# Two sums of weight blocks per MLP quad, formed by adding transfers on GpSimd in place of VectorE additions

## The chip, the cores and the metric

The kernel runs on one core of a Trainium2 chip. The metric is device time in microseconds: the median of several executions. A separate, profiled execution gives the trace. The engines are TensorE (PE; its weight loads are PEld), VectorE (DVE), ScalarE (ACT), GpSimd (POOL) and SyncE (SP). Each runs its own instructions in the order fixed at build time and waits on semaphores for the others.

## The reference, cut to what matters

A trunk of two layers works on 512 tokens of width 1024 in float32. Layer 0 mixes tokens with an mLSTM, layer 1 with a short gated convolution. Behind each mixer stands a squared-ReLU MLP with an inner width of 4096. Every part is normed before and after and added to the residual. The change touches the first matrix product of both MLPs:

```
def sqrelu_mlp(x, w_up, w_down):
    h = jax.nn.relu(x @ w_up)
    return (h * h) @ w_down
```

## The kernel before, in words

**Precision.** Every float32 factor is split into a high and a low part in the matmul's own format: `split` (L80) casts the high part on ACT (L81) and subtracts it on DVE to get the low one (L82). Each product is then three matmuls (`mm3`, L113, with the matmuls at L116 to L118): high by high, high by low, low by high.

**The up projection by quads.** `x @ w_up` is computed by a scheme of Strassen's kind that needs seven half-size products in place of eight. The rows of `w_up` (1024) are cut in two halves (`kh`), the columns into 8 groups of 512, and each group again in two halves (`nh`). One column group is a quad. It works on four blocks of 512 x 256, named in the code:

- `a` is block (0, 0), `b` is (0, 1), `c` is (1, 0) and `d` is (1, 1).

A block is 512 KB and lies in SBUF as a raw tile of 128 x 1024 (four rows of 256 columns in each partition). Raw tiles come from a pool of 7. `block` (L825) takes a raw tile and loads it from SyncE's queue (L828). `factor` (L834) takes a tile `u`, of which there are 15 for all purposes, and splits the raw tile into it. `prod` (L805) is one product of 24 matmuls of 128 x 256 into a PSUM tile `pu` (four of them). The token side of the products (`a11`, `a12`, `p1`, `r3`, `p4`, `n2`, `a22`) is prepared once per MLP by the class `Seven`.

In `run` (L854) four sums of blocks are made on DVE, in place in the raw tiles: `a + b` into `a` (L860), `b + d` into `b` (L870), then `a + d` into `a` (L877), giving a + b + d, of which the factor `w6` is made, and at last `c` added on top (L882) for the factor `w4`. Blocks `a` and `c` are also factors on their own, in `begin` (L842) and `first_done` (L849), and `d` too (L876). So `a` must have been split for the first product before the sum overwrites it, when both use the same raw tile.

**The order of the quads.** In `mlp` (L899), the first AHEAD = 3 quads are begun before their turn: their first two products (with `a` and with `c`) run from raw tiles of their own at the start of the MLP, and `run` loads the blocks again. Quads 3 to 7 are not begun: there `run` uses one raw `a` for the first product and for the sums. After quads 0 and 1, each `down(g)` (the part of the second matrix product that quad g's result feeds) alternates with the next quad. `down` accumulates in PSUM tiles `pd`, of which there are two; each result is added into SBUF by DVE (L946), or copied there by ACT when g is 0 (L944). The results of a quad's products are combined on DVE (L885 to L893), squared (L910) and split into tiles `hb`. At the end of the MLP `last_product` (L297) does the last part of the second product, and its parts on GpSimd are L338 and the power in L190.

**What orders the work.** A framework takes the instructions as the code issues them, finds the dependencies, and fixes an order for each engine when the program is built; that order need not be the code's. The constants LATE, BLOCK and PROD with `step` and `put_off` say when the transposes of a normed token tile are placed among the matmuls; the change leaves them as they are. GpSimd's queue holds, near the MLP, the power of `rstd_of` (L190), the norm gains (L177), the copies of the residual to DRAM (L796) and, before `down(5)`, the reload of that residual (L964).

Of the kernel before, what the change touches and what calls it, by code (L numbers as in the profile page):

```python
# [12 lines left out]
ALU = mybir.AluOpType  # L13

P = 128
# [25 lines left out]
def tile_hybrid_trunk(  # L41
# [15 lines left out]
    nc = tc.nc  # L57
# [10 lines left out]
    def pu():  # L68
        return psum("pu", 4)
# [24 lines left out]
    def raw_tile(shape, dtype=F32):  # L94
        return big.tile([P] + shape, dtype, tag="raw", name="raw", bufs=NRAW)
# [421 lines left out]
    def rows():  # L517
# [24 lines left out]
    a = T1[0:H, :]  # L542
    nc.vector.scalar_tensor_tensor(
        out=a, in0=thi, scalar=CAP, in1=nb, op0=ALU.mult, op1=ALU.add
# [4 lines left out]
    for c in range(NT):  # L549
# [6 lines left out]
            out=mprev[:, c + 1 : c + 2], in0=M[:, last], in1=nb[:, last], op=ALU.subtract  # L556
        )

    def by_chunk(r):
        return r.rearrange("h (c l) -> h c l", l=P)  # L560
# [3 lines left out]
        out=by_chunk(T1[32 : 32 + H, :]),  # L564
        in0=mprev[:, 0:NT].unsqueeze(2).broadcast_to([H, NT, P]),
        in1=M3,
        op=ALU.subtract,
# [3 lines left out]
        out=by_chunk(T1[96 : 96 + H, :]),  # L571
        in0=by_chunk(a),
        in1=M3[:, :, P - 1 : P].broadcast_to([H, NT, P]),
        op=ALU.subtract,
# [37 lines left out]
    for h in range(H):  # L612
# [4 lines left out]
        for c in range(NT):  # L617
# [8 lines left out]
            out=DT[:, h, :, :],  # L626
# [178 lines left out]
    def prod(o, fw, fx, first):  # L805

        for p in range(4):
            step(PROD / 4)
            for u in range(2):
                mm3(  # L810
                    o[:, u * 256 : (u + 1) * 256],
                    [fw[:, i, p, u * P : (u + 1) * P] for i in range(2)],
                    [fx[:, i, p, :] for i in range(2)],
                    first and p == 0 and u == 0,
                    p == 3,
                )

    class Quad:
# [3 lines left out]
        def __init__(self, wm, c0, c1, xT, take):  # L822
            self.wm, self.cols, self.xT, self.take = wm, (c0, c1), xT, take

        def block(self, kh, nh):  # L825
            c = self.cols[nh]
            raw = raw_tile([4, 256])
            nc.sync.dma_start(  # L828
                raw,
                self.wm[kh * 512 : (kh + 1) * 512, c : c + 256].rearrange("(p q) m -> q p m", q=P),  # L830
            )
            return raw

        def factor(self, src):  # L834
            w = unit([2, 4, 256], F32R)
            split(w[:, 0], w[:, 1], src)
            return w
# [16 lines left out]
        def run(self, begun):  # L854
            tt = nc.vector.tensor_tensor
            f = self.xT.f
            a, b = self.block(0, 0), self.block(0, 1)
            if not begun:
                self.begin(a)
            tt(out=a, in0=a, in1=b, op=ALU.add)  # L860
            w = self.factor(a)
            z = pu()
            prod(z, w, f["p1"], True)
            s1, s5 = self.s1, self.values()
            nc.scalar.copy(s5, by_tile(z))
            if not begun:
                c = self.block(1, 0)
                self.first_done(c)
            d = self.block(1, 1)
            tt(out=b, in0=b, in1=d, op=ALU.add)  # L870
            w = self.factor(b)
            y = pu()
            prod(y, w, f["r3"], True)
            s7 = self.values()
            nc.scalar.copy(s7, by_tile(y))
            w = self.factor(d)  # L876
            tt(out=a, in0=a, in1=d, op=ALU.add)  # L877
            w6 = self.factor(a)
            prod(z, w, f["p4"], False)
            if begun:  # L880
                c = self.block(1, 0)
            tt(out=a, in0=a, in1=c, op=ALU.add)  # L882
            w4 = self.factor(a)
            prod(y, w6, f["n2"], False)
            tt(out=s1, in0=by_tile(y), in1=s1, op=ALU.add)  # L885
            tt(out=s7, in0=s1, in1=s7, op=ALU.subtract)
            tt(out=s7, in0=by_tile(z), in1=s7, op=ALU.subtract)
            tt(out=s5, in0=s5, in1=s1, op=ALU.subtract)
            o = pu()
            prod(o, w4, f["a22"], True)  # L890
            self.take(1, 0, s7, None)
            self.take(1, 1, s5, None)
            tt(out=s1, in0=by_tile(o), in1=s1, op=ALU.add)  # L893
            self.take(0, 1, s1, None)

    def by_tile(o):
        return o.rearrange("p (u n) -> p u n", u=2)
# [142 lines left out]
```

## Time and profile before

| | us |
|---|---|
| median of 3 runs | 1138.42 (1138.06 to 1138.58) |
| profiled execution | 1139.16 |
| its span in the trace | 1137.4 |
| PE busy | 1098.1 (97%) |
| PEld busy | 949.2 (83%) |
| DVE busy | 733.9 (65%) |
| ACT busy | 450.2 (40%) |
| POOL busy | 64.9 (6%) |
| moved by DMA | 126.35 MB, 111 GB/s on average |

A page of the profile gives the busy time of each engine, then the span in 40 slices (one of them is 28.4 us) with a digit for the busy tenths of each, the DMA queues, the chain of work that ended last, and groups of instructions. In a group or an order of time, a row names the line of the kernel, the engine, the operation and the tiles as `out<-in`. What stands behind `<-` in brackets is what ended the idle time of the engine before that row. A busy PE need not be a PE at its peak, since matmuls are pipelined and their ends are modelled. The first MLP lies at about 244 to 560 us of the span, the second at about 785 us to the end.

### The profile page before, as it was taken

What the parts mean: (1) busy time and instruction counts of PE and PEld (TensorE: products, weight loads), DVE (VectorE), ACT (ScalarE), POOL (GpSimd) and SP (SyncE); (2) the same over time, 40 slices, a digit from 0 to 9 for tenths busy, and PEclk for the clock granted to TensorE, in tenths of its full rate; (3) what the DMA queues carried; (4) which work ended last, traced back from release to release, by engine and by line L of the source; (5) the groups of instructions that cost most, each with busy time, mean ns of one, the idle gap of its engine ahead of it and who ended that gap; (6) DMA issues with size and microseconds to landing.
All of it is one profiled execution on the core that took longest, in us unless ns stands there. A gap on an engine that the chain in (4) does not pass through costs nothing.

```text
span 1137.4 us, 15341 instructions
## 1 busy us (share of the span) xinstructions
PE 1098.1 (97%) x6243; PEld 949.2 (83%) x6243; DVE 733.9 (65%) x993; ACT 450.2 (40%) x692; POOL 64.9 (6%) x108
## 2 busy tenths in 40 slices
PE   8999999969999999999999999996999999999997
PEld 5878887869798898899889888786978889889986
DVE  5552665469776776767685444346977677676763
ACT  6431543346444244234363222234644424423421
POOL 2000100110000000000130000011000000000011
PEclk9999999989999999999999999998999999999999
DMA  8420363044353243153535331104435324315301
GB/s 263 135 67 1 101 214 93 38 158 157 117 162 96 71 130 104 64 186 103 138 88 172 113 106 59 56 37 145 151 119 160 94 74 130 104 64 185 103 28 56
DMA packets 112749, 126.35 MB, mean 111 GB/s; under 512 B 4998, under 2 KB 85158, under 8 KB 112679
## 3 DMA queue, kind: packets, MB, share of 16 engines
q1 hardware_dynamic: 109366, 113.31, 32.0%
q0 software_dynamic: 3312, 12.06, 2.9%
q8 instruction: 49, 0.80, 0.3%
q14 instruction: 22, 0.17, 0.1%
HBM read 119.07 MB, written 6.29 MB: 110 GB/s over the span
## 4 chain that ended last, share of the span: by engine, by line
PE 73%; DVE 11%; issue 9%; ACT 3%; DMA 2%; POOL 1%; SPq 0%; POOLq 0%; DVEq 0%; ACTq 0%
PE pu L116 12%; PE pu L117 12%; PE pu L118 12%; PE pd L117 11%; PE pd L118 11%; PE pd L116 11%; DVE u L82 4%; DMA raw<-in_w_in_mlstm_dram 1%; ACT u L81 1%; ACT junk L198 1%; DMA raw<-in_w_mlp_up_dram 1%; DVE t L910 1%; POOL small L190 1%; DVE u L291 1%; DVE hb L82 1%
## 5 line engine op out<-in xcount | busy, mean ns | idle before, releaser
L116 PE MATMUL pu<-u 128*128 128x256 f32 (+1 forms) x1296 | 408.2, 315 | 19.1 <-ACT u L81 18.8
L118 PE MATMUL pu<-u 128*128 128x256 f32 (+1 forms) x1296 | 403.2, 312 | 4.4 <-DVE u L82 4.4
L117 PE MATMUL pu<-u 128*128 128x256 f32 (+1 forms) x1296 | 404.8, 312 | 0.4 <-DVE u L82 0.4
L82 DVE TENSOR_TENSOR u<-raw,u 128x1024 fp32r<-128x1024 f32 (+1 forms) x248 | 295.4, 1204 | 137.7 <-ACT u L81 137.4
L81 ACT CAST u<-raw 128x1024 fp32r<-128x1024 f32 (+1 forms) x248 | 251.4, 1035 | 272.0 <-PE pd L118 118.3
L116 PEld LDWEIGHTS pu<-u 128*128 128x128 f32 x1296 | 246.0, 190 | 36.5 <-ACT u L81 20.5
L118 PEld LDWEIGHTS pu<-u 128*128 128x128 f32 x1296 | 245.1, 189 | 20.7 <-DVE u L82 6.0
L117 PEld LDWEIGHTS pu<-u 128*128 128x128 f32 x1296 | 246.0, 190 | 16.3 <-DVE u L82 1.3
L117 PE MATMUL pd<-u,hb 128*128 128x512 f32 (+1 forms) x648 | 254.2, 392 | 1.3 <-DVE u L82 1.3
L116 PE MATMUL pd<-u,hb 128*128 128x512 f32 (+1 forms) x648 | 254.5, 393 | 0.7 <-ACT u L81 0.4
L118 PE MATMUL pd<-u,hb 128*128 128x512 f32 (+1 forms) x648 | 253.9, 392 | 0.0
L117 PEld LDWEIGHTS pd<-u,hb 128*128 128x128 f32 x648 | 121.7, 188 | 30.1 <-DVE u L82 2.9
L116 PEld LDWEIGHTS pd<-u,hb 128*128 128x128 f32 x648 | 121.5, 188 | 29.3 <-DVE t L332 1.2
L118 PEld LDWEIGHTS pd<-u,hb 128*128 128x128 f32 x648 | 121.7, 188 | 28.1
L81 ACT CAST hb<-t 128x512 fp32r<-128x512 f32 x80 | 49.1, 621 | 86.1 <-DVE t L910 74.2
L946 DVE TENSOR_TENSOR u<-u,pd 128x512 f32<-128x512 f32 x80 | 54.7, 683 | 29.6 <-PE pd L118 29.5
L198 ACT ACTIVATE junk<-u 128x512 bf16<-128x512 f32 (+1 forms) x49 | 30.5, 623 | 77.7 <-DVE u L335 48.3
L82 DVE TENSOR_TENSOR hb<-t,hb 128x512 fp32r<-128x512 f32 x80 | 53.4, 687 | 3.8 <-ACT hb L81 3.6
L332 DVE TENSOR_TENSOR t<-pd,gain 128x512 f32<-128x512 f32 x16 | 11.0, 688 | 36.3 <-ACT junk L198 36.3
L964 POOL DMA_DIRECT2D u<-xd x8 | 4.3, 536 | 493.6 <-PE pu L118 493.6
L910 DVE SCALAR_TENSOR_TENSOR t<-t 128x512 f32<-128x512 f32 x48 | 31.5, 685 | 0.0
L291 DVE SCALAR_TENSOR_TENSOR u<-t,small,u 128x512 f32<-128x512 f32 (+1 forms) x33 | 22.9, 733 | 10.8 <-POOL small L190 10.8
(153 smaller groups left out, 664.8 us busy)
## 6 DMA issues: line engine op xcount, KB each, us to landing
raw<-in_w_mlp_up_dram SPq DMA_DIRECT2D x76, 512.0 KB, 3.7
raw<-in_w_mlp_down_dram SPq DMA_DIRECT2D x64, 512.0 KB, 3.5
raw<-in_w_in_mlstm_dram SPq DMA_DIRECT2D x24, 512.0 KB, 4.8
raw<-in_w_in_conv_dram SPq DMA_DIRECT2D x24, 512.0 KB, 5.3
raw<-in_w_out_mlstm_dram SPq DMA_DIRECT2D x8, 512.0 KB, 4.1
xd<-u POOLq DMA_DIRECT2D x8, 512.0 KB, 2.9
u<-xd POOLq DMA_DIRECT2D x8, 512.0 KB, 5.8
raw<-in_w_out_conv_dram SPq DMA_DIRECT2D x8, 512.0 KB, 3.5
```

Of the source, the lines that this page charges most:

```text
L81: hi = nc.scalar.copy(dst_hi, src)
L82: lo = nc.vector.tensor_tensor(out=dst_lo, in0=src, in1=dst_hi.bitcast(F32), op=ALU.subtract)
L116: nc.tensor.matmul(o, lh, rh, start=first, stop=False, skip_group_check=True)
L117: nc.tensor.matmul(o, lh, rl, start=False, stop=False, skip_group_check=True)
L118: nc.tensor.matmul(o, ll, rh, start=False, stop=last, skip_group_check=True)
L190: nc.gpsimd.tensor_tensor(out=r, in0=r, in1=mhalf[:, 0:1], op=ALU.pow)
L198: nc.scalar.activation(junk(n), src, AF.Square, scale=float(D) ** -0.5, accum_out=ms[:, i : i + 1])
L291: nc.vector.scalar_tensor_tensor(out=xt[:, hs], in0=y, scalar=r, in1=xt[:, hs], op0=ALU.mult, op1=ALU.add)
L332: nc.vector.tensor_tensor(out=yg, in0=o, in1=g[:, cs], op=ALU.mult)
L910: nc.vector.scalar_tensor_tensor(out=c, in0=o, scalar=0.0, in1=c, op0=ALU.max, op1=ALU.mult)
L946: nc.vector.tensor_tensor(out=yh, in0=yh, in1=o, op=ALU.add)
L964: nc.gpsimd.dma_start(xs[t], xd[t])
```

## The change

The sums L860 and L870 are no longer DVE additions. GpSimd issues a transfer that reads the second block from HBM once more and adds it to the raw tile: block (0, 1) onto `a`, and block (1, 1) onto `b`. The loads of `b` and `d` into raw tiles of their own remain. The sums at L877 and L882 remain on DVE. With 8 quads in each of 2 MLPs, 32 additions become 32 adding transfers of 512 KB.

```
+        def src(self, kh, nh):
+            c = self.cols[nh]
+            return self.wm[kh * 512 : (kh + 1) * 512, c : c + 256].rearrange(
+                "(p q) m -> q p m", q=P
+            )
+
         def block(self, kh, nh):
-            c = self.cols[nh]
             raw = raw_tile([4, 256])
-            nc.sync.dma_start(
-                raw,
-                self.wm[kh * 512 : (kh + 1) * 512, c : c + 256].rearrange("(p q) m -> q p m", q=P),
-            )
+            nc.sync.dma_start(raw, self.src(kh, nh))
             return raw
+
+        def plus(self, raw, kh, nh):
+            nc.gpsimd.dma_start(raw, self.src(kh, nh), accum_op=ALU.add)
...
             a, b = self.block(0, 0), self.block(0, 1)
             if not begun:
                 self.begin(a)
-            tt(out=a, in0=a, in1=b, op=ALU.add)
+            self.plus(a, 0, 1)
             w = self.factor(a)
...
             d = self.block(1, 1)
-            tt(out=b, in0=b, in1=d, op=ALU.add)
+            self.plus(b, 1, 1)
             w = self.factor(b)
```

## Prediction

> **What bounds the kernel now.** I read the page first, its busy shares and its forty slices.
>
> ```profile
> span 1137.4 us, 15341 instructions
> ...
> PE 1098.1 (97%) x6243; PEld 949.2 (83%) x6243; DVE 733.9 (65%) x993; ACT 450.2 (40%) x692; POOL 64.9 (6%) x108
> ...
> PE   8999999969999999999999999996999999999997
> ...
> DVE  5552665469776776767685444346977677676763
> ```
>
> TensorE is busy for 97% of the span, so VectorE time is worth something only near the few slices where PE falls under 9. Counted from 0, PE falls to 6 in slices 8 and 27, and DVE reaches its only 9s in the slices right behind, 9 and 28: the starts of the two MLPs. The table of windows sizes them.
>
> ```profile
> core 0: us, PE busy (x) PEld busy (x) DVE busy (x) ACT busy (x) POOL busy (x), PEclk, DMA share, GB/s
> 260.00:300.00 40.00, 36.90 (x285) 34.53 (x283) 37.73 (x49) 18.95 (x28) 0.00 (x0) 1.00 0.46 145
> 300.00:330.00 30.00, 29.43 (x168) 25.49 (x169) 19.79 (x20) 17.85 (x24) 0.00 (x0) 1.00 0.52 160
> 330.00:400.00 70.00, 70.00 (x409) 61.36 (x408) 52.57 (x64) 24.10 (x28) 0.00 (x0) 1.00 0.26 83
> 400.00:470.00 70.00, 70.00 (x463) 63.91 (x462) 52.86 (x63) 27.72 (x34) 0.00 (x0) 1.00 0.35 113
> 800.00:840.00 40.00, 37.58 (x297) 35.85 (x296) 37.73 (x50) 19.58 (x29) 0.00 (x0) 1.00 0.45 143
> 840.00:900.00 60.00, 59.34 (x327) 50.60 (x326) 43.71 (x50) 26.00 (x33) 0.00 (x0) 1.00 0.35 109
> ```
>
> In the 40 us behind each start DVE works for 37.73 us and PE idles for 3.10 and 2.42 us. In the 140 us from 330 on PE is busy for all of it and DVE for three quarters: a faster DVE gives nothing there. The chain of waits says which DVE work sets PE's pace at the first start.
>
> ```profile
> 272.25 0.15 DVE raw L860
> 272.40 0.98 issue
> 273.39 1.22 DVE raw L882
> 274.61 1.14 DVE raw L870
> 275.74 2.34 DVE u L82 x2
> ```
>
> Quad 1's two sums (L860, L870) lie in the chain, around quad 0's last sum (L882), whose factor (L82) PE is about to need.
>
> **What the change removes.** Each quad loses one L860 and one L870.
>
> ```profile
> L860 DVE TENSOR_TENSOR raw<-raw x16: 1215/1220/1226, 254.8 to 1056.2; 128x1024 f32<-128x1024 f32 x16
> L870 DVE TENSOR_TENSOR raw<-raw x16: 1218/1225/1228, 256.3 to 1058.2; 128x1024 f32<-128x1024 f32 x16
> ```
>
> That is 32 x 1.22 = 39 us of DVE, off 733.9. Almost all of it lies where PE has no idle time and pays nothing. What pays is quad 1's pair in each start: in the chain they take 0.15 + 0.98 = 1.13 us and 1.14 us, together 2.27 us, twice 4.5 us. It cannot be much more: all of PE's idle time in the four windows around the starts is 3.10 + 0.57 + 2.42 + 0.66 = 6.8 us. Behind the removed sums L82 and L882 stay next on DVE, then PE itself, so I count no more than the two pairs. Quad 0's pair stands ahead of the saturated stretch, at 254.8 and 256.3; I count it at nothing, since its replacements arrive later than it did. The loads on SP stay as they are: both blocks that are now added by a transfer are still loaded too, since later sums and factors read them.
>
> **What it adds.** 32 transfers of 512 KB on GpSimd's queue, 16.8 MB more reading. The trace has no adding transfer. The nearest rows are the plain loads that GpSimd issues (L964) and SP's loads of the same blocks.
>
> ```profile
> raw<-in_w_mlp_up_dram SPq DMA_DIRECT2D x76, 512.0 KB, 3.7
> ...
> u<-xd POOLq DMA_DIRECT2D x8, 512.0 KB, 5.8
> ```
>
> ```profile
> L964 POOL DMA_DIRECT2D u<-xd x8: 527/531/577, 489.2 to 1033.0; - x8
> ...
> DMA to landing us min/median/max: 4.0/5.8/6.8
> ```
>
> Call X the time from the issue of an adding transfer to its landing. From below, X is no less than 3.7 us, SP's load of the same block. From above, I take twice 5.8 = 11.6 us, as if reading the tile were a second transfer in series. I take 7.4: the 5.8 of GpSimd's own load, plus three more issue times of 0.53 us, since a block is 512 rows of 1 KB where that tile is 128 rows of 4 KB; it is nearest to that row. Against 1.22 us on DVE the sum thus comes some 6 us later after its inputs.
>
> The Trainium skill, DMA: Bandwidth & Descriptors, section "Anatomy of one DMA", fits a transfer from GpSimd as 2.0 us plus bytes over 436 GB/s, an estimate of 3.2 us here; the 5.8 of this trace disagrees and decides, and by 3.2 no wait below would appear and the sum would stay at -4.5 us. The Trainium skill, Collectives: The Full Stack, section "The bandwidth ceiling", speaks against the change: an adding transfer has two sources to read where a copy has one. No run here shows that yet; by it, 5.8 plus another 1.2 us for 512 KB at that rate is an estimate of 7.0, and the hold worked out below would be 1.2 us in place of 1.6.
>
> **Where the later sum is hidden.** Quads 0 to 2 were begun ahead: nothing else reads `a` before the sum, so the transfer can go as soon as the tile is in. In quads 3 to 7 the transfer into `a` must first wait until L81 and L82 have split the raw `a` for the first product. The one into `b` waits for `b` alone, no longer for L860. Quad 4 of the first MLP, on DVE:
>
> ```profile
> 380.60 1.22 DVE L82 TENSOR_TENSOR u<-raw,u 128x1024 fp32r<-128x1024 f32 x1
> ...
> 382.93 1.23 DVE L860 TENSOR_TENSOR raw<-raw 128x1024 f32<-128x1024 f32 x1
> 384.19 1.23 DVE L870 TENSOR_TENSOR raw<-raw 128x1024 f32<-128x1024 f32 x1
> 385.33 0.68 DVE L946 TENSOR_TENSOR u<-u,pd 128x512 f32<-128x512 f32 x1
> 385.93 1.22 DVE L82 TENSOR_TENSOR u<-raw,u 128x1024 fp32r<-128x1024 f32 x1
> ...
> 388.61 0.68 DVE L946 TENSOR_TENSOR u<-u,pd 128x512 f32<-128x512 f32 x1
> ...
> 393.31 0.69 DVE L946 TENSOR_TENSOR u<-u,pd 128x512 f32<-128x512 f32 x1 [1.15 <-PE pd L118]
> 396.09 0.69 DVE L946 TENSOR_TENSOR u<-u,pd 128x512 f32<-128x512 f32 x1 [2.09 <-PE pd L118]
> ...
> 399.74 0.68 DVE L946 TENSOR_TENSOR u<-u,pd 128x512 f32<-128x512 f32 x1
> ```
>
> ```profile
> 322.96 0.59 ACT L865 COPY t<-pu 128x512 f32<-128x512 f32 x1 [0.70 <-PE pu L118]
> 325.80 0.59 ACT L875 COPY t<-pu 128x512 f32<-128x512 f32 x1 [1.31 <-PE pu L118]
> ...
> 384.27 1.05 ACT L81 CAST u<-raw 128x1024 fp32r<-128x1024 f32 x1 [3.52 <-DVE raw L860]
> ```
>
> The split of `a` ends at 381.8. A transfer issued then lands at 381.8 + 7.4 = 389.2; cast (1.05) and subtraction (1.22) end at 391.5. The last of the down product's evictions is at 399.74, so the quad's products start at about 399, and the sum's product is the second of them: one product takes 325.80 - 322.96 = 2.84 us, so the factor is due at about 402. There are 10 us left: for the data alone the transfer is hidden, even at 11.6.
>
> DVE's order is less kind. Its queue runs in order, so while the subtraction of a + b waits for its cast, the evictions L946 queued behind it wait as well, and PE waits for them: `pd` has two buffers, so a group's result must be out by the time the next group ends. PE's groups end at 393.3 and 396.1, 2.8 us apart, and so, counted back, at 387.7 and 390.5. A held eviction behind the subtraction ends at 381.8 + X + 1.05 + 1.22 + 0.69 = 384.8 + X, somewhat less as DVE instructions overlap a little. If it is the eviction of the group that ends at 387.7, it is due at 390.5, and X may be 5.8 (counting 0.1 of overlap). If one more eviction stands ahead of the subtraction, it is 8.6. The order on DVE is fixed at build time and is not that of the code: L870 stands right behind L860, though the code has a factor between them. I take the kinder order, in which the framework leaves a later sum room: cost nothing. If that cover is gone, it is X - 5.8 in each of ten quads.
>
> GpSimd's queue is passed too.
>
> ```profile
> POOL u L964 <- PE pu L118: 493.6, 4, 247.0
> ```
>
> Until L964, the reload of the residual, GpSimd waits for up to 247 us at a time with nothing else to do in the MLP; quad 7's transfers come behind L964 (last at 1033.0, the last L870 at 1058.2). Nothing is held there that PE waits for.
>
> **Quad 0's start.** The first sum comes when memory is busiest (the first row is from the table of windows, with the DMA share and GB/s last; then DVE's and ACT's order of time).
>
> ```profile
> 250.00:256.00 6.00, 6.00 (x54) 6.00 (x53) 3.28 (x3) 1.70 (x3) 0.00 (x0) 1.00 1.09 360
> ```
>
> ```profile
> 254.81 1.23 DVE L860 TENSOR_TENSOR raw<-raw 128x1024 f32<-128x1024 f32 x1 [0.79 <-DMA raw<-in_w_mlp_up_dram]
> ```
>
> ```profile
> 268.82 0.58 ACT L865 COPY t<-pu 128x512 f32<-128x512 f32 x1
> ```
>
> `a` is in by 254.8, since `b` was loaded after it. With 7.4, 1.05 and 1.22 the factor is there at 264.5. Its product ended by 268.82, so it began by 266.0: just hidden, if the crowded DMA engines do not stretch X by over 1.5 us.
>
> **The sum.** -4.5 us: the profiled execution's 1139.16 us (span 1137.4 and 1.8 around it) would be 1134.7; it lies 0.7 above the median of 1138.42, against which I forecast 1133.9.
>
> **Rivals.**
> Held evictions (slower). The subtraction of a + b stands before the eviction due at 390.5, and X is 7.4: 1.6 us of PE in each of the ten quads 3 to 7, 16 us, less 4.5: 1149.9. It decides from X = 5.8 on and breaks even at 6.25. For it: DVE and ACT queues are in order, PE has no slack there, GpSimd's loads already take 5.8. Against it: ACT and DVE have idle time for another order.
> Late at the start (no change). Quad 0's sums land at X near 10 amid 360 GB/s of loads, the factors behind them on DVE and ACT shift, and the 2.27 us of each start are spent on waiting: 1138.4. For it: the DMA row above; against it: the factors of the third and fourth product have more time.
> The transfers do not add time anywhere and quad 0's pair pays as well: up to 6.8 us, 1131.6.
>
> **How the numbers follow.** Forecast 0.40, held evictions 0.37, late at the start 0.18, everything pays 0.05. A measurement of this kernel tells 0.2%, 2.3 us, from no change. Faster takes the forecast and the last rival less 0.02 for what of the forecast may fall short of 2.3 us: 0.43. That 0.02 goes half to no change (0.19) and half to slower (0.38). The range begins at 1131.6, PE's whole idle time, and goes to 1155, which is X = 7.9 in all ten held quads: (7.9 - 5.8) x 10 = 21, less 4.5, on 1138.4. A higher X with all ten held is what it leaves out. The forecast's own range is 1131.6 to 1136.
>
> **What would show it.** Right: DVE busy near 695 us, no L860 or L870 sums, PE idle about 2 us less in each start, PE still at 100% from 330 to 470, adding transfers landing in 6 to 9 us. Wrong: PE `pd` waiting on DVE L946 in the down products, one gap for each of quads 3 to 7; L82 or L81 waiting on a DMA of `raw` for several us at the start; landing times over 9 us.

## The result and the profile after

The kernel after takes 1166.25 us (median of 4 runs, 1164.72 to 1168.54), against 1138.28 us for the kernel before on the same chip: a ratio of 1.0247, 95% interval 1.0229 to 1.0265. The change makes the kernel 28 us slower. The forecast was 1133.9, and 1166.25 lies above the range's upper end of 1155.

In the profile after, the sums that stay are on other lines: the adding transfer is L837, a + d is L882 (before L877), c on top is L887 (L882), the eviction of `pd` is L951 (L946), the copies of `x` and `z` by ACT are L852 (L847) and L870 (L865). The page shows what the change was to do, and that PE pays for it.

```profile
span 1164.4 us, 15442 instructions
...
PE 1107.8 (95%) x6243; PEld 954.6 (82%) x6243; DVE 697.5 (60%) x961; ACT 448.0 (38%) x692; POOL 105.2 (9%) x140
...
PE   8999999968999999999999999996799999999997
...
DVE  5542763557775675666685444255777567566663
...
PEclk9999999988999999999999999998899999999999
```

DVE is down from 733.9 to 697.5 us and from 993 to 961 instructions: the 32 sums are gone. But span less PE busy grew from 39.3 to 56.6 us, and PE's own busy time grew by 9.7 us for the same 6243 matmuls. The row of the clock has an 8 in slices 8, 9, 27 and 28, so the clock now falls in one more slice at each start of an MLP than on the page of before:

```profile
PEclk9999999989999999999999999998999999999999
```

The windows of the prediction, after:

```profile
core 0: us, PE busy (x) PEld busy (x) DVE busy (x) ACT busy (x) POOL busy (x), PEclk, DMA share, GB/s
260.00:300.00 40.00, 32.71 (x239) 31.21 (x238) 30.75 (x39) 19.64 (x29) 1.80 (x2) 0.91 0.59 146
...
330.00:400.00 70.00, 69.38 (x435) 61.68 (x433) 44.90 (x55) 25.68 (x32) 5.13 (x4) 1.00 0.51 130
400.00:470.00 70.00, 68.31 (x445) 61.55 (x445) 46.44 (x53) 26.71 (x33) 3.85 (x3) 1.00 0.48 131
800.00:840.00 40.00, 33.44 (x243) 32.63 (x243) 24.21 (x28) 17.03 (x26) 5.20 (x4) 0.88 0.80 201
```

In the first 40 us PE does 239 matmuls where it did 285, and DVE, which was to be the bound, is busy for 30.75 in place of 37.73: nobody works, so somebody waits. From 330 to 470, where PE had been at 100%, it now idles for 2.31 us. Setting the same matmuls of the two traces side by side by their number in PE's order gives the delay at each place: 8.8 and 9.0 us arise at the two starts, and 0.9 to 1.9 us in each of quads 3 to 6 of both MLPs, eight quads, 9.3 us in all. Quad 7 loses nothing. Together that is the 27 us between the two spans.

The waits of PE name the eight in the first of these rows, which the kernel before does not have; the other two are waits at the starts:

```profile
PE pd L116 <- DVE u L951: 6.5, 8, 1.5
PE pu L116 <- ACT t L870: 4.9, 4, 1.9
PE pu L116 <- ACT t L852: 4.0, 2, 2.5
```

And ACT waits 103.3 us for the adding transfers (the last row is their time from issue to landing):

```profile
L837 POOL DMA_DIRECT2D raw<-in_w_mlp_up_dram x32: 1258/1277/1420, 253.3 to 1083.1; - x32
...
  ACT u L81: 103.3, 15
...
DMA to landing us min/median/max: 5.7/8.4/10.4
```

**The first start.** ACT and DVE in order of time:

```profile
252.99 0.59 ACT L852 COPY t<-pu 128x512 f32<-128x512 f32 x1 [0.71 <-PE pu L118]
261.64 1.04 ACT L81 CAST u<-raw 128x1024 fp32r<-128x1024 f32 x1 [8.06 <-DMA raw<-in_w_mlp_up_dram]
262.59 0.58 ACT L852 COPY t<-pu 128x512 f32<-128x512 f32 x1
264.46 1.05 ACT L81 CAST u<-raw 128x1024 fp32r<-128x1024 f32 x1 [1.30 <-DVE u L82]
265.42 0.58 ACT L247 COPY t<-pt 128x512 f32<-128x512 f32 x1
```

```profile
252.31 1.23 DVE L82 TENSOR_TENSOR u<-raw,u 128x1024 fp32r<-128x1024 f32 x1 [1.81 <-ACT u L81]
262.71 1.23 DVE L82 TENSOR_TENSOR u<-raw,u 128x1024 fp32r<-128x1024 f32 x1 [9.18 <-ACT u L81]
263.97 1.23 DVE L882 TENSOR_TENSOR raw<-raw 128x1024 f32<-128x1024 f32 x1
266.03 0.69 DVE L248 TENSOR_TENSOR t<-pt,t 128x512 f32<-128x512 f32 x1 [0.83 <-ACT t L247]
```

ACT stands for 8 us with the cast of a + b at the head of its queue, and DVE for 9 us with the subtraction behind that cast. The factor itself is ready at 263.94, where the prediction had it at 264.5: its data is on time. What is late is the rest of the two queues: a copy (L852) that must read a PSUM tile before PE adds the next product onto it, and the token side's work on the fourth token tile, whose first DVE instruction (L248) starts at 266.03, where before it started at 260.96. A second copy (L870, at 274.75) then stands on ACT behind casts that wait for the late DVE. PE waits for all of these.

```profile
263.22 0.39 PE L116 MATMUL pu<-u 128*128 128x256 f32 x1 [1.53 <-ACT t L852]
268.03 0.39 PE L116 MATMUL pu<-u 128*128 128x256 f32 x1 [1.71 <-ACT u L81]
268.84 0.38 PE L117 MATMUL pu<-u 128*128 128x256 f32 x1 [0.42 <-DVE u L82]
275.38 0.39 PE L116 MATMUL pu<-u 128*128 128x256 f32 x1 [1.86 <-ACT t L870]
```

These four gaps are 5.5 us. The kernel before has gaps in the same 40 us too: by the windows PE's idle time there grows from 3.10 to 7.29 us, which is 4.2 of the 8.8 us that the start loses. The clock takes most of the rest:

```profile
262.00:266.00 4.00, 2.78 (x23) 2.78 (x24) 2.45 (x2) 2.70 (x5) 0.00 (x0) 1.00 1.12 178
266.00:270.00 4.00, 1.87 (x14) 1.48 (x14) 3.79 (x7) 4.00 (x7) 0.00 (x0) 1.00 0.02 2
270.00:274.00 4.00, 3.53 (x18) 3.23 (x16) 4.00 (x7) 2.84 (x6) 0.00 (x0) 0.57 0.22 62
274.00:278.00 4.00, 2.62 (x17) 2.62 (x18) 4.00 (x6) 1.33 (x3) 1.27 (x1) 0.86 0.84 253
278.00:282.00 4.00, 4.00 (x28) 4.00 (x27) 2.85 (x3) 2.45 (x3) 0.00 (x0) 0.72 1.01 182
```

PE is busy for 1.87 of the 4 us from 266 on, and the granted clock is 0.57 in the next 4. In the 12 us of the last three rows it does 63 matmuls; at full speed the first start of the kernel before does 285 in 40 us, 85 in 12. In finer windows PE is busy for 1.55 of the 3.4 us from 266.6 on and for 1.64 of the 3.5 us from 273.4 on, and in the 3.4 us behind each of the two the clock is 0.50. An estimate of the loss from the last three rows is 4 x (0.43 + 0.14 + 0.28) = 3.4 us. The 1.2 us that are left arose from 244 to 250, ahead of the first adding transfer (253.32): there the clock was 0.54 on average, where it was 0.74 in the trace of before. The Trainium skill, TensorE: Matmul & The Clock Gate, section "Part 1: The HAM clock gate (the "warmup" mystery)", says that PE's clock is halved after an idle window of about 3.4 us. This trace agrees on the fall, but with no single gap over 1.71 us ahead of it.

**Quad 4 of the first MLP**, on DVE, ACT and PE:

```profile
390.31 1.22 DVE L82 TENSOR_TENSOR u<-raw,u 128x1024 fp32r<-128x1024 f32 x1
...
394.67 0.69 DVE L951 TENSOR_TENSOR u<-u,pd 128x512 f32<-128x512 f32 x1 [1.95 <-PE pd L118]
399.20 1.23 DVE L82 TENSOR_TENSOR u<-raw,u 128x1024 fp32r<-128x1024 f32 x1 [3.84 <-ACT u L81]
400.34 0.68 DVE L951 TENSOR_TENSOR u<-u,pd 128x512 f32<-128x512 f32 x1
```

```profile
398.12 2.94 ACT L81 CAST u<-raw 128x1024 fp32r<-128x1024 f32 x3 [7.67 <-DMA raw<-in_w_mlp_up_dram]
```

```profile
401.08 0.50 PE L116 MATMUL pd<-u,hb 128*128 128x512 f32 x1 [0.88 <-DVE u L951]
```

The split of `a` ended at 391.53; the transfer into `a` was issued at 392.06 and landed at 398.01, 5.95 us later. The subtraction of a + b stands ahead of an eviction; the eviction ends at 401.02, and PE, which has no third `pd`, starts its next group 0.88 us late. In quad 7 of the first MLP one more eviction (at 532.93) runs ahead of the subtraction (at 535.88), and PE loses nothing: there the order is the kind one of the prediction.

### The profile page after: what moved, and what is told of

Read it like the earlier page. It is cut to its first block, busy times and chain, and to the rows that moved or that the text cites. A ratio compares the mean times of both kernels' runs of the same rounds, so it can differ in the third digit from the quotient of the medians.

```text
span 1164.4 us, 15442 instructions
## 1 busy us (share of the span) xinstructions
PE 1107.8 (95%) x6243; PEld 954.6 (82%) x6243; DVE 697.5 (60%) x961; ACT 448.0 (38%) x692; POOL 105.2 (9%) x140
## 5 line engine op out<-in xcount | busy, mean ns | idle before, releaser
L81 ACT CAST u<-raw 128x1024 fp32r<-128x1024 f32 (+1 forms) x248 | 250.2, 1034 | 292.1 <-DMA raw<-in_w_mlp_up_dram 103.5
L116 PEld LDWEIGHTS pu<-u 128*128 128x128 f32 x1296 | 249.2, 192 | 51.0 <-ACT u L81 25.2
L117 PEld LDWEIGHTS pu<-u 128*128 128x128 f32 x1296 | 249.2, 192 | 17.7 <-DVE u L82 2.8
L118 PEld LDWEIGHTS pu<-u 128*128 128x128 f32 x1296 | 248.4, 192 | 17.0 <-DVE u L82 2.2
L837 POOL DMA_DIRECT2D raw<-in_w_mlp_up_dram x32 | 41.2, 1289 | 479.1 <-DMA raw<-in_w_mlp_up_dram 248.0
L81 ACT CAST hb<-t 128x512 fp32r<-128x512 f32 x80 | 49.0, 621 | 87.1 <-DVE t L915 75.1
L951 DVE TENSOR_TENSOR u<-u,pd 128x512 f32<-128x512 f32 x80 | 54.6, 682 | 35.9 <-PE pd L118 35.9
L190 POOL TENSOR_TENSOR small<-small,mhalf 128x1 f32<-128x1 f32 x32 | 18.7, 584 | 164.2 <-DVE small L185 154.2
```

Of the source, the lines that this page charges most:

```text
L81: hi = nc.scalar.copy(dst_hi, src)
L116: nc.tensor.matmul(o, lh, rh, start=first, stop=False, skip_group_check=True)
L117: nc.tensor.matmul(o, lh, rl, start=False, stop=False, skip_group_check=True)
L118: nc.tensor.matmul(o, ll, rh, start=False, stop=last, skip_group_check=True)
L190: nc.gpsimd.tensor_tensor(out=r, in0=r, in1=mhalf[:, 0:1], op=ALU.pow)
L837: nc.gpsimd.dma_start(raw, self.src(kh, nh), accum_op=ALU.add)
```

## The experiments

**Theory A, the in-order hold**: the cast and the subtraction of a sum are placed in the queues of ACT and DVE well before the transfer lands, and all that is queued behind them waits with them. **Theory B, the transfers themselves**: 16.8 MB more reading and 32 adding transfers slow the loads and the engines, wherever the factors stand. A further question is whether the 4.5 us of quad 1 exist.

**Where the loss lies.** Adding transfers only in quads 3 to 7 (the second kernel has `<`, quads 0 to 2), and the same condition at `b`:

```
-            self.plus(a, 0, 1)
+            if self.cols[0] >= 3 * 512:
+                self.plus(a, 0, 1)
+            else:
+                tt(out=a, in0=a, in1=b, op=ALU.add)
```

> Adding transfers only in quads 3 to 7 of each MLP (20 of the 32); quads 0 to 2 sum on VectorE as before. Theory A (in-order hold: ACT and DVE stand in their queues on the landing of the adding transfer; 8.8 us at each of the two MLP starts, from quad 0, and 1.2 us in each of quads 3 to 6, where an eviction L951 is held): 1138.3 + 8 x 1.17 = 1147.7 us. Theory B (the extra 16.8 MB of transfers crowd the DMA engines and delay all loads, so the loss goes with the number of transfers): 1138.3 + 28 x 20/32 = 1155.8 us.

> Adding transfers only in quads 0 to 2 of each MLP (12 of the 32); quads 3 to 7 sum on VectorE as before. Theory A: the two starts are lost, 1138.3 + 17.5 = 1155.8 us, and no PE wait on an eviction remains in the down products. Theory B: 1138.3 + 28 x 12/32 = 1148.8 us.

Measured: 1147.36 us (ratio 1.0084, 1.0069 to 1.0099) and 1156.19 us (1.0163, 1.0146 to 1.0181). Against 1138.05 us for the kernel before on that chip the losses are 9.3 and 18.1 us; they add up to 27.4 of the 28.0. In the first kernel all of PE's delay arises in eight steps, each at a group of `pd`.

**One of the two sums.** Only a + b by transfer, or only b + d, in all quads; the other goes back to the `tt` of before.

> Only the sum a + b is an adding transfer (16 of 32), in all quads; b + d is summed on VectorE. Theory A: quad 0's a + b is what ACT waits for first at each start, and only a's transfer must wait for the split in quads 3 to 7, so nearly all of the loss stays: 1160 to 1166 us. Theory B: half, 1152 us.

> Only the sum b + d is an adding transfer (16 of 32), in all quads; a + b is summed on VectorE. Theory A: nothing in quads 3 to 7, since b's transfer waits for b alone and lands long before it is needed; at each start some 4 to 8 us, since b + d of quad 0 is still cast early: 1146 to 1154 us, with all of it at the two starts. Theory B: half, 1152 us, spread like the transfers.

Measured: 1161.96 us (1.0217, 1.02 to 1.0234) and 1161.43 us (1.0204, 1.0189 to 1.0219). The second is a miss: b + d alone was to cost 8 to 16 us, all at the starts, and costs 23.4, almost as much as both. With a + b kept on DVE, the transfer into `b` has to wait for that sum, which reads `b` (13 of the 16 transfers wait for L865, as the first row shows), and ACT waits in its turn:

```profile
256.71 1.34 POOL L837 DMA_DIRECT2D raw<-in_w_mlp_up_dram  x1 [10.67 <-DVE raw L865]
277.18 1.29 POOL L837 DMA_DIRECT2D raw<-in_w_mlp_up_dram  x1 [19.13 <-ACT t L880]
```

```profile
263.15 1.05 ACT L81 CAST u<-raw 128x1024 fp32r<-128x1024 f32 x1 [4.40 <-DMA raw<-in_w_mlp_up_dram]
...
286.34 1.99 ACT L81 CAST u<-raw 128x1024 fp32r<-128x1024 f32 x2 [6.55 <-DMA raw<-in_w_mlp_up_dram]
```

So the kernel makes a late transfer of its own. With a + b alone the loss is still 23.9 us. Its median landing is 6.0 us in place of 8.4, but no transfer has become faster for it: those into `a` in quads 3 to 6 land in 5.7 to 6.0 us in both kernels, with nothing else in flight. What is gone are the transfers into `b`, most of which had loads in flight beside them.

**The transfer without its addition.** The order and the waits stay, but the sums a + b and b + d are left out: the transfers only copy.

```
-            nc.gpsimd.dma_start(raw, self.src(kh, nh), accum_op=ALU.add)
+            nc.gpsimd.dma_start(raw, self.src(kh, nh))
```

> As the changed kernel, but the 32 transfers on GpSimd are plain loads that overwrite the tile (the additions are left out); waits and order stay. It prices the adding by itself. Theory A with the read of the tile as the reason for the late landing: X falls from 8.4 to about 5.8 us, the holds in quads 3 to 6 vanish (threshold near 5) and each start loses 3 us less: about 1150 us. If the GpSimd queue with its 512 rows is the reason and not the adding: X stays near 8 and the time near 1166 us.

Measured: 1149.19 us (1.0095, 1.0078 to 1.0112). Its rows beside those of L837 above give the price of the addition:

```profile
L837 POOL DMA_DIRECT2D raw<-in_w_mlp_up_dram x32: 748/748/806, 253.9 to 1067.0; - x32
...
DMA to landing us min/median/max: 4.0/5.5/8.3
```

A plain copy lands in 5.5 us (median) and is issued in 0.75; the adding one takes 8.4 and 1.28. Into `a` in quads 3 to 6 it is 4.0 to 4.3 us in place of 5.7 to 6.0: with that the eight waits for an eviction go, and the 11 us that stay lie at the starts. The Trainium skill, Collectives: The Full Stack, section "The bandwidth ceiling", has an adding transfer read two sources; the 2.9 us more agree in direction.

**The traffic alone.** All sums on DVE as before; beside them the 12 adding transfers of quads 0 to 2 go to a spare block in DRAM that nobody reads.

```
-            self.plus(a, 0, 1)
+            if self.cols[0] < 3 * 512:
+                self.spare(a, 0, 1)
+            tt(out=a, in0=a, in1=b, op=ALU.add)
```

> All sums on VectorE as before, and beside them in quads 0 to 2 of each MLP the same 12 adding transfers of 512 KB, issued by GpSimd when the raw tile is in, but into a spare buffer in DRAM that nobody waits for. Theory A: traffic alone costs little, 1138 to 1141 us. Theory B: the starts lose what they lose in the kernel with adding transfers in quads 0 to 2, 1149 to 1156 us.

Measured: 1138.05 us (0.9998, 0.9989 to 1.0008), with landings of 8.3 us. The transfers at the two starts cost nothing by being there, and theory B falls for that part (with the difference that these write to DRAM and not to SBUF).

**Single quads.** The condition is now one quad, `self.cols[0] // 512 in (0,)`, or quad 1.

> Adding transfers only in quad 0 of each MLP (4 of the 32). Theory A (the loss at the starts is ACT and DVE standing on quad 0's late sums): nearly all of the 17.9 us that the kernel with quads 0 to 2 lost, 1152 to 1156 us. A rival of it (quad 1's second sum, whose tile is loaded late, holds the queues as well): a good part of the loss is not here, under 1150 us.

> Adding transfers only in quad 1 of each MLP (4 of the 32): the two sums that lay in the chain of waits of the kernel before, and the term of -4.5 us of the prediction by itself. If removing them from the saturated stretch of VectorE pays and their transfers land in time: 1133.7 us. If they hold the queues as quad 0's do: 1140 us or more. If another chain takes over at once: 1138.

Measured: 1154.52 us (1.0141, 1.0123 to 1.0159) for quad 0, and 1135.05 us (0.997, 0.9959 to 0.9982) for quad 1. Against 1138.42 us beside them, four transfers of quad 0 cost 16.1 us; four of quad 1 gain 3.4. In quad 1's kernel the two windows behind the starts read:

```profile
260.00:300.00 40.00, 37.68 (x295) 35.78 (x295) 37.18 (x50) 19.40 (x30) 2.63 (x2) 1.00 0.62 171
800.00:840.00 40.00, 38.18 (x295) 36.21 (x295) 37.18 (x50) 18.94 (x27) 2.02 (x2) 1.00 0.65 179
```

PE idles for 2.32 and 1.82 us there, before 3.10 and 2.42, and the clock stays at 1.00.

**The order at the start, first try.** Quad 0's ACT and DVE work is queued behind the last split of the token side:

```
-            split(f[:, 0, :, c], f[:, 1, :, c], src)
+            self.last = split(f[:, 0, :, c], f[:, 1, :, c], src)
...
+        hi, lo = xT.last
+        with tc.issue_after(hi), tc.issue_after(lo):
+            quads[0].run(True)
```

> As the changed kernel, but the instructions of quad 0 on ACT and DVE are queued behind the last split of the token side (t = 3), so that the splits that the first product needs do not stand behind the late sum. Theory A: most of the 17.5 us at the starts comes back, 1166 - 12 = 1154 us or less (1149 if all comes back), though quad 0's factors now come later. Theory B (late data, crowded DMA): no gain, 1166 us.

Measured: 1163.94 us (1.0213, 1.0184 to 1.0243), a miss. The split that it was tied to runs first of the last tile's splits, at 258.12, so the late cast still stood ahead of the others: the edit did not move what it should, and says nothing of the theories.

**The order at the start, second try.** Adding in quads 0 to 2; the split of `p4` is made last, and quad 0 is queued behind that one. Then the control: the same order with all sums on DVE.

```
-            split(f[:, 0, :, c], f[:, 1, :, c], src)
+            self.done = split(f[:, 0, :, c], f[:, 1, :, c], src)
...
-            self.part("p4", c, k1)
-            self.part("n2", c, k0)
             self.part("a22", c, s22)
+            self.part("n2", c, k0)
+            self.part("p4", c, k1)
...
+        hi, lo = xT.done
+        with tc.issue_after(hi), tc.issue_after(lo):
+            quads[0].run(True)
```

> As the kernel with adding transfers in quads 0 to 2 alone (1156.2 us), but quad 0's instructions on ACT and DVE are queued behind the last of the token side's splits (that of p4, now made last). Theory A: the splits no longer stand behind the late sums, some 6 us of the 8.9 us at each start come back, 1142 to 1147 us; the rest stays because quad 0's factors come later than before. If late data is the cause: 1156 us.

> All sums on VectorE as before, but with the order of the run before it: p4's split is made last for the fourth token tile and quad 0's ScalarE and VectorE work is queued behind it. If that run came within 3 us of the kernel before because the waits of quad 0's casts no longer stood ahead of the token side's work, this order in itself is worth nothing: 1136.5 to 1140.5, the same as before. If the order itself saves several us and only hides what the transfers cost, this runs under 1134.

Measured: 1141.19 us (1.0024, 1.0015 to 1.0034): of the 18.1 us of quads 0 to 2, 2.8 are left, with transfers that land in 9.2 us (median). The control is a miss, 1144.68 us (1.0053, 1.0037 to 1.0068): the order costs 6.5 us by itself. In the control quad 0's own sum has moved from 254.81, where DVE was idle, to 265.35, and PE waits for it:

```profile
267.70 0.58 PE L116 MATMUL pu<-u 128*128 128x256 f32 x1 [3.72 <-ACT u L81]
```

Of the two kernels of this order the one with the transfers is 3.5 us faster. With this order they no longer cost anything; but quad 0's first sum is due as early as DVE made it.

**Only b + d, in quads 3 to 7.**

> Only b + d of quads 3 to 7 is an adding transfer (10 of 32); all else on VectorE. Theory A: its transfer lands long before the cast, so nothing is held, and PE had no idle time there to win: 1138.3 us, no change, with 10 x 1.22 us less of DVE. Theory B: 1138.3 + 28 x 10/32 = 1147 us.

Measured: 1143.14 us (1.0044, 1.0029 to 1.0059), a miss of the same kind as b + d in all quads: the transfer into `b` waits for DVE's a + b (issued at 385.23), and the cast behind it waits 3.35 us.

**The order in quads 3 to 7, first try.** Adding in quads 3 to 7, with the factor of a + b queued behind the fifth of the eight evictions. These run on DVE, so it is the subtraction that moves; the cast on ACT stays free:

```
+            with ExitStack() as st:
+                for ins in behind:
+                    st.enter_context(tc.issue_after(ins.ins))
+                w = self.factor(a)
```

> As the kernel with adding transfers in quads 3 to 7 alone (1147.4 us), but the cast is left free and the subtraction of a + b is queued on VectorE behind the fifth of the eight evictions of the down product, where the sum has landed. Theory A (order alone; the sum is due 10 us later): the 9.3 us come back, 1138.1 us, and no PE wait on an eviction stays. If the late data itself is the cause: 1147 us.

Measured: 1157.13 us (1.016, 1.0146 to 1.0173), a miss, and worse than without the edit. DVE and ACT in quad 4:

```profile
386.35 0.69 DVE L961 TENSOR_TENSOR u<-u,pd 128x512 f32<-128x512 f32 x1 [1.95 <-PE pd L118]
391.86 1.23 DVE L82 TENSOR_TENSOR u<-raw,u 128x1024 fp32r<-128x1024 f32 x1 [4.82 <-ACT u L81]
393.00 0.68 DVE L961 TENSOR_TENSOR u<-u,pd 128x512 f32<-128x512 f32 x1
```

```profile
389.83 2.94 ACT L81 CAST u<-raw 128x1024 fp32r<-128x1024 f32 x3 [7.71 <-DMA raw<-in_w_mlp_up_dram]
```

ACT still has the cast of a + b at the head of its queue, with two other casts behind it; the subtraction of one of those now stands ahead of DVE's eviction and waits for ACT. The hold had moved from one queue to the other.

**The order in quads 3 to 7, second try.** The factors of `c` and of b + d are issued first, that of a + b behind them and behind the fifth eviction, so that both queues are free of the wait:

```
-            split(w[:, 0], w[:, 1], src)
+            self.ends = split(w[:, 0], w[:, 1], src)
...
+                c = self.block(1, 0)
+                wc = self.factor(c)
+                d = self.block(1, 1)
+                self.plus(b, 1, 1)
+                wb = self.factor(b)
+                with ExitStack() as st:
+                    for ins in behind:
+                        st.enter_context(tc.issue_after(ins.ins))
+                    for ins in self.ends:
+                        st.enter_context(tc.issue_after(ins))
+                    w = self.factor(a)
```

> Adding transfers in quads 3 to 7 alone. The casts and subtractions of c and of b + d are issued ahead of that of a + b, and that of a + b is queued behind the fifth eviction of the down product and behind the split of b + d, on ScalarE and VectorE both. In-order hold: neither queue waits for a transfer with an eviction behind it, so the 8 to 9 us of e1_late_quads go, and the time is the kernel before's, 1136 to 1140. If the adding itself, or its traffic, costs the time whatever the order: 1147, as in e1_late_quads.

Measured: 1137.57 us (0.9993, 0.9984 to 1.0003): the 9.3 us are gone, with the same 20 transfers, which land as late as before: in 5.8 to 6.1 us with nothing else in flight and 7.4 to 11.8 otherwise, where the kernel of 1147.36 us has 5.7 to 6.1 and 7.7 to 9.6. ACT waits for a transfer only where nothing else is due, and DVE not at all:

```profile
387.95 1.05 ACT L81 CAST u<-raw 128x1024 fp32r<-128x1024 f32 x1 [1.04 <-DMA raw<-in_w_mlp_up_dram]
397.05 1.05 ACT L81 CAST u<-raw 128x1024 fp32r<-128x1024 f32 x1 [8.05 <-PE pd L118]
```

```profile
388.08 0.68 DVE L973 TENSOR_TENSOR u<-u,pd 128x512 f32<-128x512 f32 x1
390.00 0.69 DVE L973 TENSOR_TENSOR u<-u,pd 128x512 f32<-128x512 f32 x1 [1.24 <-PE pd L118]
390.61 1.22 DVE L82 TENSOR_TENSOR u<-raw,u 128x1024 fp32r<-128x1024 f32 x1
```

**What of the change can stay.** Quads 1 and 2 alone; and quad 1 with quads 3 to 7 in the last order, 24 of the 32 transfers.

> Adding transfers in quads 1 and 2 alone (8 transfers). Quad 1 alone gave 1135.05. Quad 2's sums lie in the stretch where PE is busy all the time; the blocks are loaded ahead, nothing reads a before the sum, so if quad 2's cast doesn't stand waiting ahead of an eviction, it costs nothing and gives nothing: 1134.5 to 1136.5. If every later quad's transfer holds the queues as those of quads 3 to 7 do: 1.1 us more in each of two quads, 1137.3.

> Adding transfers in quad 1 and in quads 3 to 7, with the order of e14_late_order2 in the latter (24 of the change's 32 transfers). If order alone decides, quad 1's gain stays and the rest costs nothing: 1134 to 1137. If the transfers of quads 3 to 7 cost time whatever the order: about 1144.

Measured: 1135.09 us (0.9968, 0.9956 to 0.9981) and 1134.37 us (0.9965, 0.9952 to 0.9977). Both beat the kernels before and after; with quad 1 alone at 0.997 the three cannot be told apart, so the gain is quad 1's, and the other transfers neither cost nor give.

## Why the prediction was wrong, step by step

**What the change removes: right, a little too large.** Quad 1's two sums were put at 4.5 us; alone they give 3.4. The 39 us of DVE elsewhere give nothing, as argued: 8 transfers in quads 1 and 2, and 24 in quads 1 and 3 to 7, gain no more than 4 in quad 1.

**What it adds: one size for two cases, and not decisive.** X was taken as 7.4 us everywhere. Ten of the 32 transfers have nothing else in flight and land in 5.7 to 6.1 us, among them those into `a` in quads 3 to 6; the other 22 have loads or each other beside them and take 7.2 to 10.4. All lie within the bounds of 3.7 and 11.6. Where the order was changed, the same or longer landings cost little or nothing: 15 of 18 us came back at 9.2 (median), and 9.3 of 9.3 in quads 3 to 7.

**"Quad 0's start ... just hidden": the step that failed.** It was costed at nothing because the factor's data would be there at 264.5 for a product due at 266.0. The data came at 263.94, with some luck: X was 8.29 there, and the transfer went out at 253.32, 1.5 us ahead of the 254.8 that the step reckoned with. But the step asked only when the late factor is due, and not what is queued behind its cast and its subtraction, though the prediction asks just that of quads 3 to 7. On ACT that was a copy that `pu` needs before its next product, on DVE the token side's fourth tile, 5.07 us late, and PE waited for both. Quad 0's four transfers alone cost 16.1 us where the step said zero, and beside them the gain of quad 1 is lost as well: quads 0 to 2 together cost 18.1. The Trainium skill, PSUM — Partial Sum Buffer, section "Engine vs sequencer instructions", calls the queues of ScalarE and VectorE strictly first in, first out; the 5.07 us agree.

**"I take the kinder order ... cost nothing": failed too, for 9.3 us.** The framework does put the subtraction of a + b ahead of an eviction. This is the rival of held evictions, in mechanism and place; it was priced at 1.6 us in ten quads, and is 1.2 us in eight (9.3 / 8), since quad 7 loses nothing. That the price is near is in part luck: with the X of 5.95 in quad 4 the prediction's X - 5.8 would be 0.15 us. What it left out are 0.53 us from the end of the split to the issue and 0.11 from the landing to the cast (398.12); PE's gap there is 0.88.

Of the signs named for being wrong all three are there: `pd` waiting on the eviction (in four of the five quads), L81 waiting on a transfer of `raw`, and landings over 9 us.

**The rival "late at the start"** had the place right and the size wrong. It let the starts lose only the 2.27 us that they would have gained; they lose 8.8 and 9.0. Longer idle time of PE is 4.2 us of that at the first start and the fall of the clock, by the estimate above, 3.4, while the windows behind the starts in the kernel before had it at 1.00.

**The sum as it should have been**: -3.4 for quad 1, +16.1 for quad 0, +9.3 for the held evictions, and 5.4 that quads 0 to 2 lose together beyond quads 0 and 1 alone (18.1 - 16.1 + 3.4): 27.4, against 28.0 measured. What makes up the 5.4 was not taken apart. That quad 1's gain goes would follow from its source, a DVE that never pauses: behind the first start it is now busy for 30.75 of 40 us. The 0.6 that is left is less than the intervals of the ratios (about 2 us each).

What stays open: why the framework places the casts so early. That it takes an adding transfer to be shorter than it is would fit, but no run shows its reckoning. The traffic was tested by itself only at the starts; for quads 3 to 7 it is the kernel at 1137.57 us that shows no cost. The order of that kernel was not run with all sums on DVE; it could gain little by itself, since PE was busy for all of 330 to 470 before.

## What to carry to other kernels

When a piece of work moves to a slower but free resource, ask of each consumer not only when its result is due but what stands behind it in its engine's queue: a consumer that waits at the head of an in-order queue delays everything that follows. Check each queue on the way, since moving the wait out of one only shows it in the next. And move work only from where the engine is saturated: here 4 of 32 transfers carry the whole gain, and the ones from an idle engine can only lose.

## What the runs showed of the hardware

- An adding transfer of 512 KB in rows of 1 KB from GpSimd takes 1.28 us to issue. It lands in 5.7 to 6.1 us with nothing else in flight (10 of 32 in the kernel after) and in 7.2 to 10.4 with loads or others of its kind beside it. As a plain copy in the same places it takes 0.75 us to issue and lands in 4.0 to 5.8 us (median 4.1, ten of 32) and in 4.0 to 8.3.
- Twelve such transfers into DRAM at the two starts, with landings of 8.3 us, changed the time by a factor of 0.9998 (0.9989 to 1.0008).
- PE's granted clock fell to 0.50 for 3.4 us (270.0 to 273.4) after 3.4 us in which PE was busy for 1.55, with gaps of at most 1.71 us.
